# Feature-major MLP products: weights' high part against both activation parts in one 512-column pass, chunks of 256 columns

## The chip, the cores and the metric

One core of one Trainium2 chip. The metric is device time in microseconds (us), the median of several runs. PE is the matmul engine (TensorE), DVE VectorE, ACT ScalarE, POOL GpSimd, SP the engine whose queue issues the weight loads. A "pass" here is one matmul instruction: 128 x 128 weights held in the array, and so many columns streamed through them.

## The reference

A sequence of 256 tokens of width 1024 goes through a first block (mixers, then an MLP with a squared ReLU) and a second block (FFN, a hybrid mixer, FFN). The change touches the three MLP layers. Of the reference they are these lines; the rest (mixers, norms) stays as it is.

```python
x = x + jnp.square(jax.nn.relu(h @ w_mlp_in[l])) @ w_mlp_out[l]     # 1024 -> 4096 -> 1024
...
def swiglu(x, w_gate, w_up, w_down):                                 # 1024 -> 2816 -> 1024, twice
    return (jax.nn.silu(x @ w_gate) * (x @ w_up)) @ w_down
...
x = x + 0.5 * rmsnorm_2(swiglu(rmsnorm_2(x, g), w_gate, w_up, w_down), post_g)
```

All arithmetic is float32. The kernel gets that precision from fp32r matmuls by splitting each operand in a high and a low part: w·x is taken as hi·xh + hi·xl + lo·xh, three products added up in PSUM.

## The kernel before

Stages in program order: block 1's mixers, its MLP (`mlp`: W_MI, then W_MO), the first FFN (gate W_G1 and up W_U1 side by side, then down W_D1), the second mixer (`mixer2`), the second FFN (`ffn2`, the same code on W_G2, W_U2, W_D2).

**Weights.** `Wt` cuts a weight into chunks of columns (512 wide, L36) and each chunk into units of KT = 2 k-tiles, so a unit is 128 partitions x 1024 floats, 512 KB. `stream_dma` (L225) loads units in the fixed order of `plan` on SP's queue, `stream_split` (L237) makes of each raw unit a high part on ACT (L249) and a low part on DVE (L250: raw minus hi). hi and lo have 4 buffers each; a split can be issued when the last pass that reads its buffer's old content has run. `load_unit` asks for the split two units ahead and the load five ahead.

**Feature-major products** (`gemm_feat`, L320): W_MI, gate and up give their output with features on partitions and the 256 tokens as columns. For each k-tile and each 128 features f there are three passes of 256 columns: L332 (hi with xh), L334 (hi with xl), L335 (lo with xh). Two f share one PSUM bank (`acc`, [128, 2, 256]); a 512-column chunk holds two banks. As the last pass of a bank is issued, `done` takes it out: in the MLP ACT's ReLU (L990) and DVE's product with PSUM (L992), in an FFN DVE's product with the row scale rsB (L1142), ACT's SiLU (L1143) for gate, DVE's product of PSUM with it (L1147) for up; then `split_sb` makes hT's high part on ACT (L1033) and low part on DVE (L1034).

**Token-major products** (`gemm_tok`, L274): W_MO and the down products put the two token halves t = 0 and t = 1 in two banks of their own, 512 columns each: L288 (hi with h's high part), L289 (lo), L290 (hi with h's low part). For down's second chunk the last two units are run for t = 0 first and then for t = 1 (`tail=2`), so that t = 0's exit (ACT's squares L397, DVE's L1087) runs beside t = 1's passes.

**PSUM.** In these stages `banks(acc=6, tr=2)` gives six one-bank tiles for accumulators and two for transposes. A tile is taken again when all readers of its old content are through.

**Order.** SP's and POOL's orders are as written. PE, DVE and ACT are ordered by the scheduler, which interleaves neighbouring chunks where the code allows it. Each engine executes its instructions in order and stops at the first one whose wait is not met. The FFN's gate needs rsB, which at the first FFN comes out of a chain behind W_MO (x2 L1003, its squares L397, xf L1021, a Newton square root, two transposes); until rsB is there gate's results stay in PSUM.

Of the kernel before, what the change touches and what calls it, by code (L numbers as in the profile page):

```python
# [22 lines left out]
KT = 2  # L23
# [12 lines left out]
def widths_of(n):  # L36
    return [512] * (n // 512) + ([n % 512] if n % 512 else [])


class Wt:  # L40


    def __init__(self, name, k, widths):
        self.name, self.k, self.widths = name, k, widths
        self.kt = k // 128
        self.off, o = [], 0
        for w in widths:
            row = []
            for u in range(0, self.kt, KT):
                n = min(KT, self.kt - u)  # L50
# [51 lines left out]
W_MI = Wt("w_mlp_in", D, [512] * 8)  # L102
W_MO = Wt("w_mlp_out", 4096, [512] * 2)
FFW = widths_of(FF2)
W_G1 = Wt("ffn1_w_gate_2", D, FFW)
W_U1 = Wt("ffn1_w_up_2", D, FFW)
# [5 lines left out]
W_G2 = Wt("ffn2_w_gate_2", D, FFW)  # L112
W_U2 = Wt("ffn2_w_up_2", D, FFW)
# [81 lines left out]


class Prog:
# [8 lines left out]
    def plan(self):  # L206

        o = [(W_IN1, c) for c in (4, 0, 1, 3, 2, 5, 6, 7, 8)]
        for c in range(2):
            o += [(W_BRB, c), (W_BRA, c)]  # L210
        o += [(W_OUT1, 0), (W_OUT1, 1)]
        o += [(W_MI, c) for c in range(8)] + [(W_MO, 0), (W_MO, 1)]
# [24 lines left out]
    def stream_split(self, upto):  # L237

        nc = self.nc
        while self.n_split <= min(upto, len(self.units) - 1):  # L240
# [5 lines left out]
            hi = self.wh.tile([128, KT * 512], F32R, tag="hi", name="hi")  # L246
            lo = self.wl.tile([128, KT * 512], F32R, tag="lo", name="lo")
# [26 lines left out]
    def gemm_tok(self, W, c, xh, xl, done, head=0, tail=0, mid=None, late=None, rate=1, delay=0, acc=None):  # L274
# [5 lines left out]
        acc = acc or (lambda: self.pacc.tile([128, 512], F32, tag="acc", name="acc"))  # L280
        ps = [acc() for _ in range(2)]
# [152 lines left out]
    def run(self):  # L434
# [9 lines left out]
        with ExitStack() as es:  # L444
# [43 lines left out]
            with self.banks(acc=6, tr=2):  # L488
                self.ffn2(x)
# [482 lines left out]
    def mlp(self, x1):  # L972
# [11 lines left out]
        with tc.tile_pool(name="mlph", bufs=1) as hp, tc.tile_pool(name="mlpt", bufs=2) as tp:  # L984
            hT = [hp.tile([128, 32, 256], F32R, name="hT%d" % i) for i in range(2)]

            def hdone(c):
# [7 lines left out]
            for c in range(8):  # L995
                self.gemm_feat(W_MI, c, *self.x1T, hdone(c), delay=1, rate=2)
# [132 lines left out]
    def ffn(self, x, xT, rs, WG, WU, WD, gi, name, final=False):  # L1129
# [3 lines left out]
        with tc.tile_pool(name=name + "h", bufs=1) as hp, tc.tile_pool(name=name + "t", bufs=2) as tp:  # L1133
# [3 lines left out]
            for c, w in enumerate(FFW):  # L1137
                sg = {}
# [10 lines left out]
                self.gemm_feat(WG, c, *xT, gdone, delay=1, rate=2)  # L1149
                self.gemm_feat(WU, c, *xT, udone)  # L1150
# [389 lines left out]
```

## Time and profile before

| | us |
|---|---|
| median of 3 runs (least, most) | 1147.55 (1147.12, 1147.79) |
| the profiled execution | 1146.21 |
| its span in the trace | 1144.4 |
| PE busy in the span | 1117.1 |
| DVE busy | 733.1 |
| ACT busy | 553.6 |

The profile's page gives busy times and the chain of work that ended last; the trace gives groups of instructions by line (mean duration of one), a timeline (start, duration, and in brackets how long the engine had been idle and who released it), and busy time by stretches with the granted clock of PE (PEclk: 1.00 is 2.4 GHz, 0.50 is 1.2 GHz). In the trace's time the stages lie so: W_MI from 235 to 328, W_MO to 416, gate and up of the first FFN to 544, its down to 604, the second mixer to 945, gate and up of the second FFN from 948.5 to 1078, its down to 1138, the end at 1144.4. PE's matmuls are pipelined: the duration of one (0.28 us for 256 columns) is longer than the spacing of two, and the spacing is what a stream of them costs.

### The profile page before, as it was taken

What the parts mean: (1) busy time and instruction counts of PE and PEld (TensorE: products, weight loads), DVE (VectorE), ACT (ScalarE), POOL (GpSimd) and SP (SyncE); (2) the same over time, 40 slices, a digit from 0 to 9 for tenths busy, and PEclk for the clock granted to TensorE, in tenths of its full rate; (3) what the DMA queues carried; (4) which work ended last, traced back from release to release, by engine and by line L of the source; (5) the groups of instructions that cost most, each with busy time, mean ns of one, the idle gap of its engine ahead of it and who ended that gap; (6) DMA issues with size and microseconds to landing.
All of it is one profiled execution on the core that took longest, in us unless ns stands there. A gap on an engine that the chain in (4) does not pass through costs nothing.

```text
span 1144.4 us, 19495 instructions
## 1 busy us (share of the span) xinstructions
PE 1117.1 (98%) x7808; PEld 1042.9 (91%) x7808; DVE 733.1 (64%) x1155; ACT 553.6 (48%) x818; POOL 137.0 (12%) x141
## 2 busy tenths in 40 slices
PE   8987999999999999999999999999999999999997
PEld 8886899899998899999888999889999988999986
DVE  5855676766664567565557776556779777656553
ACT  6323444465553455444446335545555456444452
POOL 0411130000000000000000775000323000000000
PEclk9998999999999999999999999999999999999999
DMA  8794213655555556564754655434545565655662
GB/s 288 258 169 104 74 57 129 202 170 185 185 189 192 186 189 196 185 185 149 222 182 157 215 170 177 163 130 147 181 146 161 162 193 172 186 184 156 211 188 89
DMA packets 57035, 197.03 MB, mean 172 GB/s; under 512 B 6828, under 2 KB 7100, under 8 KB 56688
## 3 DMA queue, kind: packets, MB, share of 16 engines
q1 hardware_dynamic: 53856, 186.44, 51.1%
q0 software_dynamic: 2800, 9.21, 3.5%
q8 instruction: 61, 1.00, 0.4%
q14 instruction: 30, 0.25, 0.1%
q10 hardware_dynamic: 288, 0.14, 0.1%
HBM read 192.84 MB, written 1.44 MB: 170 GB/s over the span
## 4 chain that ended last, share of the span: by engine, by line
PE 84%; POOL 5%; DMA 5%; DVE 4%; ACT 1%; issue 1%; DVEq 0%; POOLq 0%; ACTq 0%
PE acc L332 16%; PE acc L334 16%; PE acc L335 16%; PE acc L288 9%; PE acc L290 9%; PE acc L289 9%; DMA BT<-tvd 2%; PE sm L799 2%; POOL sw L1219 2%; POOL qkT L1220 2%; DMA sw<-qkT 2%; PE o L832 1%; POOL qkT L1218 1%; DVE lo L250 1%; PE o L1341 1%
## 5 line engine op out<-in xcount | busy, mean ns | idle before, releaser
L250 DVE TENSOR_TENSOR lo<-raw,hi 128x1024 fp32r<-128x1024 f32 (+3 forms) x364 | 451.3, 1243 | 296.2 <-ACT hi L249 293.6
L249 ACT ACTIVATE hi<-raw 128x1024 fp32r<-128x1024 f32 (+3 forms) x364 | 373.0, 1026 | 446.7 <-PE acc L334 244.3
L332 PE MATMUL acc<-xh,hi 128*128 128x256 f32 x1656 | 470.9, 286 | 0.6 <-ACT hi L249 0.6
L334 PE MATMUL acc<-xl,hi 128*128 128x256 f32 x1656 | 471.0, 285 | 0.0
L335 PE MATMUL acc<-xh,lo 128*128 128x256 f32 x1656 | 469.4, 285 | 0.1
L332 PEld LDWEIGHTS acc<-xh,hi 128*128 128x128 f32 x1656 | 317.5, 192 | 4.4 <-issue 2.5
L334 PEld LDWEIGHTS acc<-xl,hi 128*128 128x128 f32 x1656 | 318.4, 192 | 2.4 <-issue 2.0
L335 PEld LDWEIGHTS acc<-xh,lo 128*128 128x128 f32 x1656 | 317.4, 192 | 1.6 <-issue 1.0
L290 PE MATMUL acc<-hi,hT 128*128 128x512 f32 x304 | 118.5, 390 | 0.0
L289 PE MATMUL acc<-lo,hT 128*128 128x512 f32 x304 | 118.3, 389 | 0.0
L288 PE MATMUL acc<-hi,hT 128*128 128x512 f32 x304 | 117.7, 389 | 0.0
L289 PEld LDWEIGHTS acc<-lo,hT 128*128 128x128 f32 x304 | 57.1, 188 | 11.9
L290 PEld LDWEIGHTS acc<-hi,hT 128*128 128x128 f32 x304 | 57.1, 188 | 11.9
L288 PEld LDWEIGHTS acc<-hi,hT 128*128 128x128 f32 x304 | 57.0, 188 | 11.4
L288 PE MATMUL acc<-hi,xh 128*128 128x386 f32 (+1 forms) x128 | 48.2, 378 | 0.9 <-ACT xh L366 0.9
L289 PE MATMUL acc<-lo,xh 128*128 128x386 f32 (+1 forms) x128 | 47.6, 372 | 0.0
L290 PE MATMUL acc<-hi,xl 128*128 128x386 f32 (+1 forms) x128 | 47.0, 373 | 0.2 <-DVE xl L367 0.2
L1038 POOL DMA_DIRECT2D row<-in_rows x4 | 2.3, 576 | 293.2 <-DVE xf L1021 214.0
L810 ACT ACTIVATE L<-L,nn 128x256 f32<-128x256 f32 (+1 forms) x48 | 21.3, 444 | 25.8 <-DVE nn L808 22.4
L288 PEld LDWEIGHTS acc<-hi,xh 128*128 128x128 f32 x128 | 24.0, 188 | 4.4 <-ACT xh L366 1.2
L290 PEld LDWEIGHTS acc<-hi,xl 128*128 128x128 f32 x128 | 24.0, 188 | 3.7 <-DVE xl L367 0.8
L289 PEld LDWEIGHTS acc<-lo,xh 128*128 128x128 f32 x128 | 24.1, 188 | 2.4
(414 smaller groups left out, 1260.1 us busy)
## 6 DMA issues: line engine op xcount, KB each, us to landing
raw<-in_w_in SPq DMA_DIRECT2D x100, 512.0 KB, 3.6
raw<-in_ffn_w_down SPq DMA_DIRECT2D x44, 512.0 KB, 4.1
raw<-in_ffn_w_gate SPq DMA_DIRECT2D x40, 512.0 KB, 3.5
raw<-in_ffn_w_up SPq DMA_DIRECT2D x40, 512.0 KB, 3.5
raw<-in_w_mlp_in SPq DMA_DIRECT2D x32, 512.0 KB, 4.2
raw<-in_w_mlp_out SPq DMA_DIRECT2D x32, 512.0 KB, 3.5
raw<-in_w_out SPq DMA_DIRECT2D x16, 512.0 KB, 3.5
raw<-in_w_in SPq DMA_DIRECT2D x16, 386.0 KB, 3.3
```

The lines of the kernel that those rows point to most:

```text
L249: nc.scalar.activation(hi[:, :n * w], raw[:, :n * w], AF.Copy)
L250: nc.vector.tensor_tensor(lo[:, :n * w], raw[:, :n * w], hi[:, :n * w], op=ALU.subtract)
L288: nc.tensor.matmul(ps[t][:, :w], xh[:, k, sl], hi, start=(k == 0), stop=False)
L289: nc.tensor.matmul(ps[t][:, :w], xh[:, k, sl], lo, start=False, stop=False)
L290: nc.tensor.matmul(ps[t][:, :w], xl[:, k, sl], hi, start=False, stop=last)
L332: nc.tensor.matmul(o, hi[:, fs], xh[:, k, :], start=(k == 0 and f % 2 == 0), stop=False, skip_group_check=True)
L334: nc.tensor.matmul(o, hi[:, fs], xl[:, k, :], start=False, stop=False, skip_group_check=True)
L335: nc.tensor.matmul(o, lo[:, fs], xh[:, k, :], start=False, stop=last, skip_group_check=True)
L799: nc.tensor.matmul(ps[:, i, :], q[pr:pr + 64, U["fts"][i], t * 128:t * 128 + 128], kk, start=True, stop=True)
L810: nc.scalar.activation(L[:, i, :], L[:, i, :], AF.Exp, bias=nn[:, i:i + 1], scale=1.0, accum_out=lsum[:, t, br, h:h + 1])
L1219: nc.gpsimd.tensor_tensor(sw, sw, bc4(1), op=ALU.mult)
L1220: nc.gpsimd.tensor_tensor(q[0:32], q[0:32], sw, op=ALU.add)
```

## The change

W_MI, gate and up use a new function, `gemm_pair`, in the place of `gemm_feat` (which stays for the mixers). The two parts of the activations now lie side by side in one tile `xs` [128, 8, 2, 256] (`Parts`), so hi can meet both in one pass of 512 columns (L368); lo with xh stays a pass of 256 columns (L369). The accumulator is a tile of two banks, one for each f; within a bank the first 256 columns collect hi·xh + lo·xh and the others hi·xl. At the exit ACT copies the second halves to an SBUF tile `sum` (L373), DVE adds the first halves (L374), and the old steps work on `sum`. Chunks are 256 columns wide and units four k-tiles of 256 columns, so the bytes of a unit and the number of units stay. In these stages all accumulators are two-bank tiles, three of them; `gemm_tok` takes t = 0 and t = 1 as the two banks of one tile. `sum` and `sg` have two buffers each.

```diff
-W_MI = Wt("w_mlp_in", D, [512] * 8)
+W_MI = Wt("w_mlp_in", D, [256] * 16, 4)
-FFW = widths_of(FF2)
+FFW = [256] * (FF2 // 256)
...
+class Parts:
+    def __init__(self, both):
+        self.both = both
+        self.hi, self.lo = both[:, :, 0, :], both[:, :, 1, :]
...
     def gemm_tok(...)
-        acc = acc or (lambda: self.pacc.tile([128, 512], F32, tag="acc", name="acc"))
-        ps = [acc() for _ in range(2)]
+        if self.pair:
+            ps = self.pacc.tile([128, 2, 512], F32, tag="acc", name="acc")
+            ps = [ps[:, 0, :], ps[:, 1, :]]
+        else:
+            acc = acc or (lambda: self.pacc.tile([128, 512], F32, tag="acc", name="acc"))
+            ps = [acc() for _ in range(2)]
...
+    def gemm_pair(self, W, c, x, done, rate=1, delay=0):
+        nc = self.nc
+        ps = self.pacc.tile([128, 2, 512], F32, tag="acc", name="acc").rearrange("p f (a t) -> p f a t", a=2)
+        for u in range(len(W.off[c])):
+            for k, hi, lo in self.load_unit(W, c, u):
+                last = k == W.kt - 1
+                for f in range(2):
+                    fs = slice(f * 128, f * 128 + 128)
+                    nc.tensor.matmul(ps[:, f, :, :], hi[:, fs], x.both[:, k, :, :], start=(k == 0), stop=False)
+                    nc.tensor.matmul(ps[:, f, 0, :], lo[:, fs], x.hi[:, k, :], start=False, stop=last)
+                if delay <= k < W.kt - 1:
+                    self.flush(rate)
+        s = self.sump.tile([128, 2, 256], F32, tag="sum", name="sum")
+        nc.scalar.activation(s, ps[:, :, 1, :], AF.Copy)
+        nc.vector.tensor_tensor(s, ps[:, :, 0, :], s, op=ALU.add)
+        done(s)
...
-            with self.banks(acc=6, tr=2):
+            with self.banks(acc=3, tr=2, pair=True):
...
-                def f(i, ps):
-                    r = tp.tile([128, 2, 256], F32, tag="r", name="r")
-                    nc.scalar.activation(r, ps, AF.Relu)
+                def f(p):
                     h = tp.tile([128, 2, 256], F32, tag="h", name="h")
-                    nc.vector.tensor_tensor(h, ps, r, op=ALU.mult)
-                    self.split_sb(h, hT, 4 * c + 2 * i)
+                    nc.vector.scalar_tensor_tensor(h, p, 0.0, p, op0=ALU.max, op1=ALU.mult)
+                    self.split_sb(h, hT, 2 * c)
...
-                def gdone(i, ps):
-                    s = sg[i] = tp.tile([128, 2, 256], F32, tag="s%d" % i, name="s")
-                    nc.vector.tensor_tensor(s, ps, bc2, op=ALU.mult)
-                    nc.scalar.activation(s, s, AF.Silu)
+                def gdone(p):
+                    nc.vector.tensor_tensor(p, p, bc2, op=ALU.mult)
+                    nc.scalar.activation(sg, p, AF.Silu)
-                def udone(i, ps):
+                def udone(p):
                     h = tp.tile([128, 2, 256], F32, tag="h", name="h")
-                    nc.vector.tensor_tensor(h, ps, sg[i], op=ALU.mult)
-                    self.split_sb(h, hT, 4 * c + 2 * i)
+                    nc.vector.tensor_tensor(h, p, sg, op=ALU.mult)
+                    self.split_sb(h, hT, 2 * c)
```

How the change moves instructions is seen at three places. The first is PE's order in the first FFN's gate and up, at the join of two chunks. In the rows of before acc_4560 is the second bank of the first up chunk (u0) and acc_4689 the first bank of the second gate chunk.

```order
L332 MATMUL acc_4560<-xh_3731,hi_4591 128x256
L334 MATMUL acc_4560<-xl_3732,hi_4591 128x256
L335 MATMUL acc_4560<-xh_3731,lo_4592 128x256
L332 MATMUL acc_4689<-xh_3731,hi_4621 128x256 [waits Activation_49]
L334 MATMUL acc_4689<-xl_3732,hi_4621 128x256
L335 MATMUL acc_4689<-xh_3731,lo_4622 128x256
```

After, two such joins in PE's order. acc_4290 is the second gate chunk (g1), acc_4340 the second up chunk (u1, in the tile that held g0), acc_4393 the third gate chunk (g2), acc_4443 the third up chunk (u2, in the tile that held g1).

```order
L368 MATMUL acc_4290<-xs_3489,hi_4260 128x512
L369 MATMUL acc_4290<-xs_3489,lo_4261 128x256
L368 MATMUL acc_4340<-xs_3489,hi_4291 128x512 [waits DVE_49]
L369 MATMUL acc_4340<-xs_3489,lo_4292 128x256
...
L368 MATMUL acc_4393<-xs_3489,hi_4363 128x512
L369 MATMUL acc_4393<-xs_3489,lo_4364 128x256
L368 MATMUL acc_4443<-xs_3489,hi_4394 128x512 [waits DVE_49,PE_49]
L369 MATMUL acc_4443<-xs_3489,lo_4395 128x256
```

Three passes for a weight tile became two, and the first pass of u1 and of u2 now waits for DVE, where before it waited for ACT's split alone. The second place is DVE's order at the same point of the program, from the split before rsB on. Before (acc_4403 and acc_4404 are the first gate chunk's two banks, s its scaled copies):

```order
L250 TENSOR_TENSOR lo_4692<-raw_4595,hi_4691 128x1024 [waits DMAHW6_49,PE_49,Activation_49]
L513 COPY rsB_4394<-tr_4485 128x256 [waits PE_49]
L1142 TENSOR_TENSOR s_4547<-acc_4403,rsB_4394 128x512 [waits DVE_49]
L1142 TENSOR_TENSOR s_4556<-acc_4404,rsB_4394 128x512
L250 TENSOR_TENSOR lo_4722<-raw_4625,hi_4721 128x1024 [waits DMAHW7_49,PE_49,Activation_49]
L1147 TENSOR_TENSOR h_4675<-acc_4559,s_4547 128x512 [waits Activation_49]
L1147 TENSOR_TENSOR h_4685<-acc_4560,s_4556 128x512 [waits Activation_49]
```

After (sum_4232 is g0's sum, sum_4282 u0's, sum_4335 g1's; lo_4467 goes into the buffer that g2's last pass reads):

```order
L263 TENSOR_TENSOR lo_4445<-raw_4367,hi_4444 128x1024 [waits DMAHW0_49,Activation_49]
L1178 TENSOR_TENSOR sum_4232<-sum_4232,rsB_4149 128x512 [waits DVE_49]
L263 TENSOR_TENSOR lo_4467<-raw_4398,hi_4466 128x1024 [waits DMAHW1_49,PE_49,Activation_49]
L1183 TENSOR_TENSOR h_4285<-sum_4282,sg_4158 128x512 [waits Activation_49]
L374 TENSOR_TENSOR sum_4335<-acc_4290,sum_4335 128x512 [waits DVE_49,Activation_49]
L1178 TENSOR_TENSOR sum_4335<-sum_4335,rsB_4149 128x512 [waits DVE_49]
```

The read that frees g1's accumulator (L374) stands behind the split lo_4467 and behind h; before, the reads that free the gate's banks stood right behind rsB. The third place is PE's order at the end of the first FFN's down product, where the passes for t = 0 end and those for t = 1 begin. Before:

```order
L288 MATMUL acc_6093<-hi_6239,hT0_4401 128x512
L289 MATMUL acc_6093<-lo_6240,hT0_4401 128x512
L290 MATMUL acc_6093<-hi_6239,hT1_4402 128x512
L288 MATMUL acc_6094<-hi_6221,hT0_4401 128x512
L289 MATMUL acc_6094<-lo_6222,hT0_4401 128x512
```

After:

```order
L305 MATMUL acc_5536<-hi_5681,hT0_4156 128x512
L306 MATMUL acc_5536<-lo_5682,hT0_4156 128x512
L307 MATMUL acc_5536<-hi_5681,hT1_4157 128x512
L305 MATMUL acc_5536<-hi_5663,hT0_4156 128x512 [waits DVE_49]
L306 MATMUL acc_5536<-lo_5664,hT0_4156 128x512
```

The order of the passes is the same, but both halves are one tile now, and the first pass for t = 1 waits for a read of t = 0's half by DVE. The same wait stands in the second FFN's down product. At W_MO's end the scheduler put the last three t = 1 passes, which have this wait too, behind 26 passes of the first FFN.

## Rows read from the trace of the kernel before

**Rows 1.** The page, part 1: engine, busy us, share of the span, instructions.

```profile
PE 1117.1 (98%) x7808; PEld 1042.9 (91%) x7808; DVE 733.1 (64%) x1155; ACT 553.6 (48%) x818; POOL 137.0 (12%) x141
```

**Rows 2.** Windows by stage: us, busy by engine, PEclk, DMA share, GB/s.

```profile
235.00:328.00 93.00, 93.00 (x776) 92.96 (x777) 58.42 (x67) 51.85 (x69) 0.00 (x0) 1.00 0.57 183
416.00:544.00 128.00, 128.00 (x1069) 128.00 (x1069) 82.11 (x117) 64.26 (x82) 0.65 (x2) 1.00 0.56 178
544.00:604.00 60.00, 60.00 (x267) 49.62 (x266) 31.11 (x33) 27.01 (x34) 0.00 (x0) 1.00 0.64 200
948.50:1078.20 129.70, 129.70 (x1069) 129.70 (x1070) 79.72 (x105) 64.80 (x82) 0.00 (x0) 0.99 0.56 173
```

**Rows 3.** Timeline of PE in gate and up: start us, duration us, engine, line.

```profile
460.78 0.28 PE L334 MATMUL acc<-xl,hi 128*128 128x256 f32 x1
...
461.74 0.28 PE L332 MATMUL acc<-xh,hi 128*128 128x256 f32 x1
```

**Rows 4.** Timeline of PE in the first down product, 512 columns.

```profile
579.66 0.39 PE L290 MATMUL acc<-hi,hT 128*128 128x512 f32 x1
...
581.02 0.39 PE L290 MATMUL acc<-hi,hT 128*128 128x512 f32 x1
```

**Rows 5.** Groups by line and shape: busy us, mean ns of one, idle before.

```profile
L250 DVE TENSOR_TENSOR lo<-raw,hi 128x1024 fp32r<-128x1024 f32 x324 | 411.4, 1272 | 270.0 <-ACT hi L249 267.6 <-PE acc L335 0.6 <-PE sm L363 0.6
L249 ACT ACTIVATE hi<-raw 128x1024 fp32r<-128x1024 f32 x324 | 343.2, 1060 | 407.0 <-PE acc L334 220.6 <-PE acc L290 113.2 <-issue 47.9
L1147 DVE TENSOR_TENSOR h<-acc,s 128x512 f32<-128x512 f32 x22 | 15.1, 689 | 2.7 <-PE acc L335 1.7 <-ACT s L1143 0.7
L990 ACT ACTIVATE r<-acc 128x512 f32<-128x512 f32 x16 | 9.4, 589 | 10.3 <-PE acc L335 10.3
```

**Rows 6.** Timeline of ACT and DVE as the first FFN's first SiLU comes.

```profile
440.22 1.06 ACT L249 ACTIVATE hi<-raw 128x1024 fp32r<-128x1024 f32 x1 [2.26 <-PE acc L334]
441.30 1.28 ACT L1143 ACT_TABLE_LOAD   x1
442.60 1.15 ACT L1143 ACTIVATE s<-s 128x512 f32<-128x512 f32 x2
...
441.32 1.23 DVE L250 TENSOR_TENSOR lo<-raw,hi 128x1024 fp32r<-128x1024 f32 x1 [0.44 <-ACT hi L249]
```

**Rows 7.** Timeline at the first FFN's start, DVE's chain towards rsB.

```profile
415.54 1.40 DVE L1003 SCALAR_TENSOR_TENSOR x<-acc,r,x 128x512 f32<-128x512 f32 x2
...
424.50 2.48 DVE L1021 SCALAR_TENSOR_TENSOR xf<-x,rf,row 128x1024 f32<-128x1024 f32 x2
```

**Rows 8.** Timeline at the end of the first down product.

```profile
600.97 0.39 PE L288 MATMUL acc<-hi,hT 128*128 128x512 f32 x1
...
601.17 0.69 ACT L397 ACTIVATE junk<-acc,rsf 128x512 bf16<-128x512 f32 x1 [1.87 <-PE acc L290]
...
602.06 0.74 DVE L1087 SCALAR_TENSOR_TENSOR f<-acc,rsf,row 128x512 f32<-128x512 f32 x1
```

**Rows 9.** Timeline at the end of the second down product.

```profile
1135.35 0.39 PE L288 MATMUL acc<-hi,hT 128*128 128x512 f32 x1
...
1136.44 0.74 DVE L1087 SCALAR_TENSOR_TENSOR f<-acc,n_r,row 128x512 f32<-128x512 f32 x1
```

**Rows 10.** Timeline at the start of the second mixer.

```profile
605.04 0.44 PE L288 MATMUL acc<-hi,xh 128*128 128x386 f32 x1 [0.86 <-ACT xh L366]
...
605.76 0.34 DVE L367 SCALAR_TENSOR_TENSOR xl<-acc,cols,xh 128x128 fp32r<-128x128 f32 x1
...
607.89 0.33 PE L363 MATMUL tr<-ident,xn 128*128 128x128 f32 x1 [0.39 <-DVE xn L1104]
```

**Rows 11.** Windows around pauses of PE: us, PE busy, then the clock as PEclk.

```profile
945.00:948.50 3.50, 1.39 (x7) 0.62 (x6) 3.46 (x10) 2.24 (x9) 0.64 (x2) 1.00 0.58 206
949.40:952.70 3.30, 3.30 (x18) 3.30 (x17) 2.70 (x6) 2.00 (x4) 0.00 (x0) 0.50 0.06 22
...
603.90:607.90 4.00, 2.51 (x14) 1.71 (x12) 3.66 (x10) 2.84 (x8) 0.00 (x0) 1.00 0.01 2
607.90:611.00 3.10, 3.10 (x19) 2.60 (x20) 2.67 (x8) 2.01 (x6) 1.51 (x3) 1.00 0.56 191
```

More of the change, by code (lines that the diff above doesn't have):

```diff
@@ L48, in __init__ @@
             row = []
-            for u in range(0, self.kt, KT):
-                n = min(KT, self.kt - u)
+            for u in range(0, self.kt, kts):
+                n = min(kts, self.kt - u)
                 row.append((o, u, n))
@@ L211, in plan @@
         o += [(W_OUT1, 0), (W_OUT1, 1)]
-        o += [(W_MI, c) for c in range(8)] + [(W_MO, 0), (W_MO, 1)]
+        o += [(W_MI, c) for c in range(len(W_MI.widths))] + [(W_MO, 0), (W_MO, 1)]
         def ffn(g, u, d):
@@ L231, in stream_dma @@
             w = W.widths[c]
-            raw = self.wr.tile([128, KT * 512], F32, tag="raw", name="raw")
+            raw = self.wr.tile([128, UNIT], F32, tag="raw", name="raw")
             nc.sync.dma_start(raw[:, :n * w], self.ap[W.name][o:o + 128 * n * w].rearrange("(p f) -> p f", p=128))
@@ L380, in new_xT @@
     def new_xT(self):
-        return (self.xtp.tile([128, 8, 256], F32R, tag="xh", name="xh"),
-                self.xtp.tile([128, 8, 256], F32R, tag="xl", name="xl"))
+        return Parts(self.xtp.tile([128, 8, 2, 256], F32R, tag="xs", name="xs"))
     def held(self, on):
@@ L416, in banks @@
     @contextmanager
-    def banks(self, acc, tr, sm=0, o=0):
+    def banks(self, acc, tr, sm=0, o=0, pair=False):
+        self.pair = pair
         with ExitStack() as es:
@@ L487, in run @@
             self.dump("x4", x)
-            with self.banks(acc=6, tr=2):
+            with self.banks(acc=3, tr=2, pair=True):
                 self.ffn2(x)
@@ L985, in mlp @@
             hT = [hp.tile([128, 32, 256], F32R, name="hT%d" % i) for i in range(2)]
+            self.sump = tp
             def hdone(c):
-                def f(i, ps):
-                    r = tp.tile([128, 2, 256], F32, tag="r", name="r")
-                    nc.scalar.activation(r, ps, AF.Relu)
+                def f(p):
                     h = tp.tile([128, 2, 256], F32, tag="h", name="h")
-                    nc.vector.tensor_tensor(h, ps, r, op=ALU.mult)
-                    self.split_sb(h, hT, 4 * c + 2 * i)
-                return f
-            for c in range(8):
-                self.gemm_feat(W_MI, c, *self.x1T, hdone(c), delay=1, rate=2)
+                    nc.vector.scalar_tensor_tensor(h, p, 0.0, p, op0=ALU.max, op1=ALU.mult)
+                    self.split_sb(h, hT, 2 * c)
+                return f
+            for c in range(len(W_MI.widths)):
+                self.gemm_pair(W_MI, c, self.x1T, hdone(c), delay=1, rate=2)
             xT = self.new_xT()
@@ L1136, in ffn @@
             bc2 = rsB.unsqueeze(1).to_broadcast([128, 2, 256])
-            for c, w in enumerate(FFW):
-                sg = {}
-                def gdone(i, ps):
-                    s = sg[i] = tp.tile([128, 2, 256], F32, tag="s%d" % i, name="s")
-                    nc.vector.tensor_tensor(s, ps, bc2, op=ALU.mult)
-                    nc.scalar.activation(s, s, AF.Silu)
-                def udone(i, ps):
+            self.sump = tp
+            for c in range(len(FFW)):
+                sg = tp.tile([128, 2, 256], F32, tag="sg", name="sg")
+                def gdone(p):
+                    nc.vector.tensor_tensor(p, p, bc2, op=ALU.mult)
+                    nc.scalar.activation(sg, p, AF.Silu)
+                def udone(p):
                     h = tp.tile([128, 2, 256], F32, tag="h", name="h")
-                    nc.vector.tensor_tensor(h, ps, sg[i], op=ALU.mult)
-                    self.split_sb(h, hT, 4 * c + 2 * i)
-                self.gemm_feat(WG, c, *xT, gdone, delay=1, rate=2)
-                self.gemm_feat(WU, c, *xT, udone)
+                    nc.vector.tensor_tensor(h, p, sg, op=ALU.mult)
+                    self.split_sb(h, hT, 2 * c)
+                self.gemm_pair(WG, c, xT, gdone, delay=1, rate=2)
+                self.gemm_pair(WU, c, xT, udone)
             return self.down_post(WD, hT, gi, x, 0.5, name, rs, None if final else self.g["mix_pre_g_2"])
```

25 lines of the change are left out of this document (14 added, 11 removed).

## The prediction, made before the changed kernel ran

> **What bounds the kernel now.** I read the page's busy times first: PE is busy 98% of the span, DVE and ACT about two thirds and half of it [rows 1]. Shares over the span hide stages, so the windows by stage come next: in W_MI, in gate and up of both FFNs and in the first down product PE is busy in every microsecond, at full clock, while DVE has a third of its time free and ACT nearly half, at 173 to 200 GB/s of weights [rows 2]. So there the price is PE's spacing of passes, not a split or a load, and only two things can move the end: fewer PE nanoseconds, or a new wait of PE that no other passes cover.
>
> **What it removes.** Nine passes in PE's timeline of gate and up show 8 spacings in 461.74 - 460.78 = 0.96 us: 0.120 us for 256 columns [rows 3]. Seven 512-column passes show 6 spacings in 581.02 - 579.66 = 1.36: 0.227 us [rows 4]. Two 256-column passes cost 0.240, one of 512 costs 0.227: each pass has about 13.3 ns that don't grow with its columns (256 columns at 2.4 GHz are 106.7 ns). A weight tile cost 3 x 0.120 = 0.360 us and will cost 0.227 + 0.120 = 0.347. W_MI has 8 k-tiles x 32 groups of 128 features = 256 of them, each FFN 8 x 44 = 352, in all 960: **-12.8 us**. That is all there is to gain, since the columns streamed stay the same.
>
> The Trainium skill ("TensorE: Matmul & The Clock Gate", section Back-to-back issue gap) speaks against this: it gives an isolated pass N/2.4 + 2.5 ns, so a fixed part of 2.5 ns instead of 13.3. By that the merged pass would save about 2.4 us, an estimate from the Trainium skill's figure, and the sum below would be 10.4 us worse. Its other figure, 131 ns for 512 columns in a stream, is contradicted here by 227 ns [rows 4]. The rival on the saving below takes it up from rows.
>
> **What it adds on ACT and DVE.** Per chunk of 256 columns one ACT copy out of PSUM (nearest row: ReLU from PSUM, 0.59 us) and one DVE add of the same shape as h (0.69) [rows 5]. A gate chunk with its up chunk takes PE 32 x 0.347 = 11.1 us; in it DVE has 4 splits at 1.27 and five 512-wide operations at 0.69, 8.5 us, and ACT 4 splits at 1.06 and four operations of about 0.6, 6.6 us [rows 5]. Both fit, with a quarter of DVE's time free. Units stay 512 KB and come every 2.78 us, as slow as in the down products, so loads cost nothing. With three two-bank tiles a chunk's exit has the next two chunks' passes, 11.1 us, before its tile is wanted; it takes 0.59 + 0.69 plus one split (1.27) that may stand ahead. In the steady stream I charge nothing; if that cover were gone, each of 60 chunks could pay up to 1.3 us.
>
> **Where it adds waits that nothing covers.** By the order, at three kinds of places.
>
> (a) First FFN's start, first passes of g1. The scheduler runs g0, u0 and g1 interleaved, and puts W_MO's last three t = 1 passes among them. g1's first low part goes into the buffer that W_MO's last pass frees; from then on hi 1.06, lo 1.27 and handoffs of 0.15 are needed [rows 5], 2.5 us, while about 10 passes (1.7 us) stand between. Stall 0.8 us; ends 0 and 2.5.
>
> (b) u1's first pass wants g0's tile. DVE's read of it (L374) stands behind a split whose buffer is freed by g0's last pass: hi 1.06, lo 1.27, sum 0.69 and 0.28 of handoffs, 3.3 us [rows 5], against 8 passes or 1.4 us. At least 1.9 us. DVE also has the chain towards rsB here, x2 and xf of 1.40 and 2.48 us [rows 7], which comes later than before because W_MO's end is late; I take 2.5, ends 1.9 and 5.
>
> (c) u2's first pass wants g1's tile, and there is no pass between g2's last one and it. DVE's read of g1 stands behind the split lo_4467 (freed by that last pass) and behind h, which needs SiLU. On ACT follow one another: hi 1.06, the table load 1.28, SiLU 0.58 [rows 6], the copy of g1 0.59; then DVE's sum 0.69 [rows 5]; with five handoffs of 0.06, 4.5 us, all of it stall. Ends: 3 (if the copy or the load comes earlier in time) and 6.
>
> In the trace the SiLU starts 20 ns after the table load ends, and the load has 1.28 us [rows 6]. The Trainium skill ("ScalarE: Activation LUTs", section What ACT_TABLE_LOAD costs) has the load at 1283 ns, which the row confirms, and a drain of about 1380 ns besides, which the row doesn't show ahead of SiLU; by the Trainium skill (c) would be 1.4 us longer and the whole about 1150.0.
>
> (d) The ends of the two down products. t = 0 and t = 1 are one tile now, and t = 1's first pass waits for DVE's read of t = 0. In the trace it starts at 600.97, ACT's squares at 601.17 and DVE's read L1087 from 602.06 to 602.80 [rows 8]: with 0.05 for the handoff 602.85 - 600.97 = 1.88 us. The second FFN's has the same shape, 1135.35 to 1136.44 + 0.74 + 0.05 [rows 9]: 1.88. The exit behind it follows PE in both, so nothing takes it back: **3.8 us**. (A wait for ACT's squares alone would give 0.9 each.)
>
> (e) Starts of the second mixer and the second FFN. The first passes there wait for DVE's low part, not ACT's high part. In the mixer the first pass starts at 605.04 and the low part that it would wait for ends at 606.10, 1.1 us later; but PE waits at 607.89 for xn all the same [rows 10], which swallows most of it. I take 0.2 and for the FFN 0.3, ends 0 and 1.7 together.
>
> (f) The clock. After the 3.5 us around 945 in which PE was busy for 1.39, the granted clock went to 0.50 for 3.3 us; after 4 us with 2.51 busy it stayed at 1.00 [rows 11]. The stall of 4.5 us in (c) is more like the first: 3.3 us at half rate lose 1.65. I charge one, **1.7 us**; ends 0 and 5.
>
> **Sum.** -12.8 + 0.8 + 2.5 + 4.5 + 3.8 + 0.5 + 1.7 = +1.0 us. The profiled execution took 1146.2 and its span 1144.4, the median is 1147.55, 1.3 above the former; a difference carries over, so 1147.3 for an execution like it and **1148.6 us** for the median. All low ends at once (0, 1.9, 3.0, 1.8, 0, 0) give 1141.4, all high ones (2.5, 5, 6, 3.8, 1.7, 5) 1158.7. One of (b), (c) and (f) at an end moves the sum by 1.5 to 3.3, so the forecast's own range is 1145.3 to 1150.5.
>
> **Rivals.**
> *Slower, the start of the first FFN decides.* One engine queue holds splits, sums and the chain to rsB. If W_MO's late end delays x2 and xf, each 2.48 us of xf stands ahead of the sum for u1, and (b) and (a) pause PE long enough for the clock too. Price: two more half-rate stretches of 1.65, 3.3 us more, about 1152. For it: PE is the only engine that has no slack and its pauses follow each other within 20 us. Against: after 1.5 us of idle within 4 us the clock held [rows 11]. It decides from about 2.3 us over the forecast's waits.
> *Faster, the waits are half.* I read the waits at the FFN's start off the order; a wait on an engine counts everything before it, and if splits get ahead in time because ACT and DVE have free time, (a) to (c) and the clock cost 4 to 5 us less: about 1144.5. For it: a quarter of DVE's time is free. Against: buffers freed by PE's own last passes fix (b) and (c).
> *All waits hidden.* Only the -12.8 and perhaps the tails: 1134.8 to 1138.5. Against: the tile shared by t = 0 and t = 1 can't be hidden by anything in the rows.
> *The saving is not there.* If the fixed 13 ns goes with the switch of weights and a 512-column pass followed by a 256-column one waits for it differently than in equal streams, the 12.8 shrinks to 2 or so: 1159. Rows 3 and 4 show only streams of equal passes. The gap rule of the Trainium skill, cited above, leads to the same time.
>
> **Chances.** Forecast 0.48 (1145.3 to 1150.5); slower start 0.25 (1150.5 to 1154); half waits 0.15; all hidden 0.05; saving not there 0.07. 0.2% is 2.3 us, about what a measurement here can tell from none: same lies between 1145.25 and 1149.85. Slower: 0.24 + 0.07 + 0.06 of the forecast's own upper end, 0.37. Faster: 0.13 + 0.05 + 0.03, 0.21. Same 0.42. The range from 1141.5 to 1154.0 leaves out the last two rivals and an edge of the others.
>
> **What would show it.** Spacing of PE in gate and up of 0.227 and 0.120 alternately, and W_MI's window shorter by 256 x 13.3 ns = 3.4 us, the second FFN's gate and up by 4.7. At the first FFN's start idle times of PE ahead of L368, released by DVE's L374, of about 2.5 and 4.5 us, and a stretch at 0.50 behind the second. In both down products an idle of 1.9 us ahead of L305, released by DVE. DVE's and ACT's own durations as before. I am wrong if the alternating spacing is above 0.36 us for a pair, if PE idles in the steady stream, or if the first FFN's start loses under 4 or over 12 us.

## The result and the profile after

The changed kernel took 1152.25 us (median of 15 runs), the kernel before 1145.47 (15 runs): ratio 1.0066, 95% interval 1.0050 to 1.0081. It is slower by two thirds of a per cent. The time lies inside the wide range of the prediction (1141.5 to 1154.0), but above the forecast's own 1145.3 to 1150.5, where the rival "slower, the start of the first FFN decides" lies. The likeliest case, no change that can be told, is not what came.

The profiled execution took 1152.25 with a span of 1150.5. Its busy times, which answer to [rows 1]:

```profile
PE 1114.8 (97%) x6848; PEld 995.0 (86%) x6848; DVE 769.6 (67%) x1207; ACT 573.0 (50%) x854; POOL 137.0 (12%) x141
```

PE has 960 instructions less and is busy 2.3 us less, but the span is 6.0 us longer. A table of the stages, each from its first pass to the next stage's first pass, shows where (us; the last column is the best version of the experiments below):

| stage | before | after | best |
|---|---|---|---|
| W_MI | 92.9 | 89.6 | 89.9 |
| W_MO | 88.1 | 87.4 | 88.1 |
| first FFN, gate and up | 128.0 | 136.3 | 125.2 |
| first down, to the mixer's first pass | 61.2 | 64.4 | 61.2 |
| second mixer | 343.4 | 345.1 | 344.5 |
| second FFN, gate and up | 129.7 | 127.0 | 126.7 |
| second down, to the start of its last pass | 59.6 | 61.7 | 59.6 |
| from there to the end of the span | 6.6 | 7.1 | 7.1 |
| sum from W_MI's start | 909.5 | 918.5 | 902.4 |

In the column "after" three passes of W_MO, 0.8 us with their pause, are counted with gate and up. From W_MI's start on the changed kernel is 9.0 us longer; block 1 ahead of it, in code that is the same, happened to be 3 us shorter in this execution (more on that at the last experiment).

Windows by stage (us, busy by engine, PEclk, DMA share, GB/s), which answer to [rows 2] and [rows 11]:

```profile
232.00:321.50 89.50, 89.50 (x518) 78.36 (x519) 68.51 (x83) 51.46 (x69) 0.00 (x0) 1.00 0.59 189
409.00:545.00 136.00, 129.32 (x719) 111.58 (x718) 96.95 (x136) 74.49 (x99) 0.65 (x2) 0.97 0.54 176
954.70:1081.60 126.90, 126.90 (x717) 110.36 (x717) 92.53 (x120) 74.02 (x97) 0.00 (x0) 0.99 0.56 183
441.90:446.30 4.40, 0.08 (x1) 0.00 (x0) 2.63 (x5) 4.21 (x6) 0.00 (x0) 0.90 0.64 189
446.40:452.20 5.80, 5.80 (x18) 4.93 (x19) 4.36 (x7) 2.75 (x5) 0.00 (x0) 0.50 0.08 33
```

W_MI and the second FFN are still full of PE. The first FFN's gate and up has 6.7 us without PE, and PE ran at 0.50 of its clock for 5.8 us behind a pause of 4.4 us. PE's waits (us in total, times, longest) name the releasers:

```profile
PE acc L368 <- DVE sum L374: 6.0, 2, 4.4
PE acc L305 <- DVE f L1123: 3.4, 2, 1.7
...
PE acc L305 <- DVE xs L403: 2.0, 1, 2.0
```

These are the predicted waits: L368 on DVE's read of an accumulator twice, the two down products' t = 1 passes on DVE's read of t = 0, and the second mixer's first pass on DVE's instruction for the low part (L403; what it waits for there is taken up below, at (e)). The longest, in the timeline of PE, DVE and ACT:

```profile
439.81 0.42 DVE L549 COPY rsB<-tr 128x256 f32<-128x256 f32 x1 [1.67 <-PE tr L548]
...
441.70 0.28 PE L369 MATMUL acc<-xs,lo 128*128 128x256 f32 x1
446.39 0.77 PE L368 MATMUL acc<-xs,hi 128*128 128x512 f32 x1 [4.42 <-DVE sum L374]
...
442.98 1.23 DVE L263 TENSOR_TENSOR lo<-raw,hi 128x1024 fp32r<-128x1024 f32 x1 [1.02 <-ACT hi L262]
444.92 0.69 DVE L1183 TENSOR_TENSOR h<-sum,sg 128x512 f32<-128x512 f32 x1 [0.72 <-ACT sg L1179]
445.55 0.69 DVE L374 TENSOR_TENSOR sum<-acc,sum 128x512 f32<-128x512 f32 x1
...
441.89 1.06 ACT L262 ACTIVATE hi<-raw 128x1024 fp32r<-128x1024 f32 x1 [2.19 <-PE acc L368]
442.97 1.28 ACT L1179 ACT_TABLE_LOAD   x1
444.26 0.63 ACT L1179 ACTIVATE sg<-sum 128x512 f32<-128x512 f32 x1
444.92 0.60 ACT L373 ACTIVATE sum<-acc 128x512 f32<-128x512 f32 x1
```

g2's last pass starts at 441.70, u2's first at 446.39: 4.69 us where a spacing is 0.12, so 4.57 lost. Between them stand, one behind the other, hi, the table load, SiLU, h beside the copy of g1, and DVE's sum, as (c) had them. The pause of the first down product, which answers to [rows 8]:

```profile
602.14 0.39 PE L307 MATMUL acc<-hi,hT 128*128 128x512 f32 x1
...
603.45 0.74 DVE L1123 SCALAR_TENSOR_TENSOR f<-acc,rsf,row 128x512 f32<-128x512 f32 x1
...
604.25 0.50 PE L305 MATMUL acc<-hi,hT 128*128 128x512 f32 x1 [1.73 <-DVE f L1123]
```

2.11 us from pass to pass instead of 0.227: 1.88 lost, the second down product's 2.11 (1138.56 to 1140.67) the same.

What the merged pass gave is read from starts of passes far apart. In W_MI, 58 pairs of a 512 and a 256 pass, and in the first FFN 57:

```profile
269.85 0.40 PE L368 MATMUL acc<-xs,hi 128*128 128x512 f32 x1
...
289.96 0.40 PE L368 MATMUL acc<-xs,hi 128*128 128x512 f32 x1
```

```profile
479.83 0.40 PE L368 MATMUL acc<-xs,hi 128*128 128x512 f32 x1
...
499.97 0.40 PE L368 MATMUL acc<-xs,hi 128*128 128x512 f32 x1
```

20.11 / 58 = 346.7 ns, as predicted, and 20.14 / 57 = 353.3 ns. Three passes of 256 cost 360 [rows 3]. So W_MI saves 13.3 ns for a weight tile, the FFNs (the second has 353 as well) only 6.7.

### The profile page after: what moved, and what is told of

It is laid out like the page before. It is cut to its first block, busy times and chain, and to the rows that moved or that the text cites. A ratio compares the mean times of both kernels' runs of the same rounds, so it can differ in the third digit from the quotient of the medians.

```text
span 1150.5 us, 17641 instructions
## 1 busy us (share of the span) xinstructions
PE 1114.8 (97%) x6848; PEld 995.0 (86%) x6848; DVE 769.6 (67%) x1207; ACT 573.0 (50%) x854; POOL 137.0 (12%) x141
## 4 chain that ended last, share of the span: by engine, by line
PE 84%; POOL 5%; DMA 4%; DVE 4%; ACT 2%; issue 1%; DVEq 0%; SPq 0%; POOLq 0%; ACTq 0%
PE acc L368 19%; PE acc L369 10%; PE acc L305 9%; PE acc L306 9%; PE acc L307 9%; PE acc L349 6%; PE acc L351 6%; PE acc L352 6%; PE sm L835 2%; POOL sw L1255 2%; DMA sw<-qkT 2%; POOL qkT L1256 2%; DMA BT<-tvd 1%; PE o L868 1%; POOL qkT L1254 1%; DVE lo L263 1%
## 5 line engine op out<-in xcount | busy, mean ns | idle before, releaser
L263 DVE TENSOR_TENSOR lo<-raw,hi 128x1024 fp32r<-128x1024 f32 (+2 forms) x356 | 450.7, 1269 | 270.9 <-ACT hi L262 268.9
L262 ACT ACTIVATE hi<-raw 128x1024 fp32r<-128x1024 f32 (+2 forms) x356 | 371.1, 1044 | 439.1 <-issue 132.7
L368 PE MATMUL acc<-xs,hi 128*128 128x512 f32 x960 | 342.6, 401 | 6.2 <-DVE sum L374 6.0
L369 PE MATMUL acc<-xs,lo 128*128 128x256 f32 x960 | 270.1, 282 | 0.7 <-DVE lo L263 0.7
L368 PEld LDWEIGHTS acc<-xs,hi 128*128 128x128 f32 x960 | 181.9, 190 | 50.5 <-issue 4.7
L349 PE MATMUL acc<-xs,hi 128*128 128x256 f32 (+1 forms) x696 | 199.7, 288 | 0.3 <-ACT hi L262 0.3
L351 PE MATMUL acc<-xs,hi 128*128 128x256 f32 (+1 forms) x696 | 198.9, 287 | 0.0
L352 PE MATMUL acc<-xs,lo 128*128 128x256 f32 (+1 forms) x696 | 198.0, 287 | 0.1
L369 PEld LDWEIGHTS acc<-xs,lo 128*128 128x128 f32 x960 | 182.9, 191 | 1.3 <-DVE lo L263 1.0
L349 PEld LDWEIGHTS acc<-xs,hi 128*128 128x128 f32 (+1 forms) x696 | 133.4, 192 | 3.7 <-issue 2.5
L351 PEld LDWEIGHTS acc<-xs,hi 128*128 128x128 f32 (+1 forms) x696 | 133.7, 192 | 2.4 <-issue 2.0
L352 PEld LDWEIGHTS acc<-xs,lo 128*128 128x128 f32 (+1 forms) x696 | 132.9, 192 | 1.6 <-issue 1.0
L305 PE MATMUL acc<-hi,hT 128*128 128x512 f32 x304 | 118.7, 391 | 3.4 <-DVE f L1123 3.4
L305 PEld LDWEIGHTS acc<-hi,hT 128*128 128x128 f32 x304 | 57.1, 188 | 16.1 <-DVE f L1123 4.3
L306 PEld LDWEIGHTS acc<-lo,hT 128*128 128x128 f32 x304 | 57.1, 188 | 11.7
L305 PE MATMUL acc<-hi,xs 128*128 128x386 f32 (+1 forms) x128 | 48.6, 381 | 2.1 <-DVE xs L403 2.0
L374 DVE TENSOR_TENSOR sum<-acc,sum 128x512 f32<-128x512 f32 x60 | 41.1, 684 | 0.0
```

What stands on the lines that cost most here:

```text
L262: nc.scalar.activation(hi[:, :n * w], raw[:, :n * w], AF.Copy)
L263: nc.vector.tensor_tensor(lo[:, :n * w], raw[:, :n * w], hi[:, :n * w], op=ALU.subtract)
L305: nc.tensor.matmul(ps[t][:, :w], xh[:, k, sl], hi, start=(k == 0), stop=False)
L306: nc.tensor.matmul(ps[t][:, :w], xh[:, k, sl], lo, start=False, stop=False)
L349: nc.tensor.matmul(o, hi[:, fs], xh[:, k, :], start=(k == 0 and f % 2 == 0), stop=False, skip_group_check=True)
L351: nc.tensor.matmul(o, hi[:, fs], xl[:, k, :], start=False, stop=False, skip_group_check=True)
```

## The experiments

Four edits of the changed kernel alone, run side by side; then two combinations, one narrower edit, and the kernel before once more. Medians are of 6 to 15 runs. The versions did not all run on the same chip, so each ratio is against the kernel before on its own chip.

| version | median us | ratio, 95% interval |
|---|---|---|
| changed kernel | 1152.25 | 1.0066, 1.0050 to 1.0081 |
| two tiles in three places | 1139.96 | 0.9951, 0.9933 to 0.9968 |
| four buffers for sum | 1146.22 | 1.0003, 0.9986 to 1.0020 |
| order 512, 512, 256, 256 | 1149.72 | 1.0031, 1.0017 to 1.0044 |
| merged pass undone | 1156.26 | 1.0090, 1.0066 to 1.0114 |
| two tiles for W_MO alone | 1144.09 | 0.9992, 0.9974 to 1.0009 |
| two tiles, order 512, 512, 256, 256 | 1136.32 | 0.9918, 0.9898 to 0.9938 |
| all three edits | 1137.58 | 0.9925, 0.9896 to 0.9953 |

**Two tiles for the two token halves.** In the second chunk of W_MO and of both down products:

```diff
-            ps = self.pacc.tile([128, 2, 512], F32, tag="acc", name="acc")
-            ps = [ps[:, 0, :], ps[:, 1, :]]
+            ps = [self.pacc.tile([128, 2, 512], F32, tag="acc", name="acc") for _ in range(1 + c)]
+            ps = [ps[0][:, 0, :], ps[c][:, 1 - c, :]]
```

> The changed kernel with one edit: in the second chunk of W_MO and of the down products, the token halves t = 0 and t = 1 lie in two accumulator tiles instead of in the two banks of one. Theory (a tile is one unit for waits): the idle of 1.88 us ahead of the first t = 1 pass goes in both down products, 3.8 us of the span, and at W_MO's end the last three t = 1 passes stand where they stood before, with no pause among the first FFN's first passes (0.95 us today). Total 3 to 5 us shorter than the changed kernel, about 1148. Rival (the exit behind the last pass, not the wait, sets the end; or two tiles more in use delay the next chunk): the idle moves to the first passes of the next chunk or to the exit, and the total stays within 1 us of 1152.

It took 12.3 us off, not 3 to 5. The waits of L305 on DVE's f are gone, as expected (2.0 us each with the passes' slow start), and the mixer's first pass waits for ACT's high part again:

```profile
PE acc L368 <- DVE sum L374: 1.0, 1, 1.0
PE acc L305 <- ACT xs L402: 0.9, 1, 0.9
```

But the first row shows more: of the 6.0 us of PE's waits for DVE's reads at the first FFN's start 1.0 is left. Gate and up took 127.0 us (417.57 to 544.52) where the changed kernel had 136.3, and no stretch is at 0.50. So 8.5 us of the first FFN's loss (136.3 less W_MO's 0.8, less 127.0) hung on the shared tile as well. The expectation had missed that; which of the three places does it is the question of the fifth experiment.

**Four buffers for sum** in the FFNs:

```diff
-        with ... as hp, tc.tile_pool(name=name + "t", bufs=2) as tp:
+        with ... as hp, tc.tile_pool(name=name + "t", bufs=2) as tp, \
+                tc.tile_pool(name=name + "s", bufs=4) as sp:
...
-            self.sump = tp
+            self.sump = sp
```

> The changed kernel with one edit: the tile sum has four buffers in the FFNs instead of two. In the changed kernel PE waits 4.58 us at 441.7 for DVE's read of the second gate chunk's accumulator. Theory A (the buffers): that read can't be issued because the sum's two buffers are held by the first gate and up chunks until rsB has come; with four buffers it is done long before, the idle of 4.6 us goes, and with it the 5.7 us at half clock behind it (2.6 to 3 us lost); total about 7.5 us shorter, near 1144.7. Theory B (the prediction's: the splits in front of it in DVE's queue and ACT's table load): the splits and the load stay, so at least 2 us of the idle stays and the half clock may too; total 0 to 3 us shorter.

6.0 us off by the medians; gate and up took 129.0 us instead of 136.3, and the pause of 4.6 us and the half clock are gone: theory A. DVE's reads of g0, u0 and g1 (L374) now stand ahead of rsB in time, where the changed kernel had g1's at 445.55, 5.7 us behind rsB:

```profile
426.91 0.68 DVE L374 TENSOR_TENSOR sum<-acc,sum 128x512 f32<-128x512 f32 x1
428.71 0.69 DVE L374 TENSOR_TENSOR sum<-acc,sum 128x512 f32<-128x512 f32 x1
430.51 0.69 DVE L374 TENSOR_TENSOR sum<-acc,sum 128x512 f32<-128x512 f32 x1
...
438.54 0.42 DVE L549 COPY rsB<-tr 128x256 f32<-128x256 f32 x1
```

The splits, the table load and SiLU are still there; PE just doesn't wait for them. So what the prediction called the cause of (c), a split and the table load in front of the read, only set how long after rsB the read came. That it had to come after rsB is due to two buffers, both held by sums that wait for rsB.

**Another order of the passes:** both of 512 columns of a k-tile, then both of 256.

```diff
                     nc.tensor.matmul(ps[:, f, :, :], hi[:, fs], x.both[:, k, :, :], start=(k == 0), stop=False)
+                for f in range(2):
+                    fs = slice(f * 128, f * 128 + 128)
                     nc.tensor.matmul(ps[:, f, 0, :], lo[:, fs], x.hi[:, k, :], start=False, stop=last)
```

> The changed kernel with the four passes of a k-tile in another order: both 512-column passes first, then both of 256 columns. In the changed kernel a 512 and a 256 pass together take 346.7 ns in W_MI, as predicted, but 353.3 in both FFNs. Theory A (the extra 6.6 ns come from alternating the two lengths): in this order the pair costs 227 + 120 = 347 ns everywhere, the FFNs give 704 x 6.6 = 4.7 us. Theory B (they come from the stage, by what it reads, or by the state in which the stream was left by a stall): 353 ns stay in the FFNs and 347 in W_MI, total unchanged within 1.5 us.

2.5 us off by the medians, 4.0 by the ratios. A pair costs 348.3 to 348.6 ns in all three stages in this order, so neither theory holds whole: the FFNs gain 5 ns for a pair (704 x 5 = 3.5 us), W_MI loses 1.6 (0.4 us). The other half of theory B, the state in which the stream was left by a pause, gets its evidence from the two-tile version, where the alternating order stayed. There W_MI's 57 pairs, the same instructions in the same order as in the changed kernel, took this:

```profile
269.78 0.40 PE L368 MATMUL acc<-xs,hi 128*128 128x512 f32 x1
...
289.92 0.40 PE L368 MATMUL acc<-xs,hi 128*128 128x512 f32 x1
```

20.14 / 57 = 353.3 ns. So it is not the stage: the alternating stream has two rhythms, 346.7 and 353.3. In each of the four profiles with that order the rhythm changed only where something broke the alternation, and then held, for up to 100 us. That can be a pause or a few transposes, but also two passes of one length in a row, with PE never idle. In the two-tile version's second FFN six pairs from 955.85 to 957.97 took 353.3 ns each; then the scheduler put passes of one length side by side at several places, with no idle time of PE, and the 18 pairs behind them took 6.24 us, 346.7 ns each:

```profile
958.32 0.64 PE L368 MATMUL acc<-xs,hi 128*128 128x512 f32 x2
...
965.33 0.39 PE L368 MATMUL acc<-xs,hi 128*128 128x512 f32 x1
...
971.57 0.39 PE L368 MATMUL acc<-xs,hi 128*128 128x512 f32 x1
```

What picks a rhythm at such a place is not settled.

**The merged pass undone alone**, all else as changed:

```diff
-                    nc.tensor.matmul(ps[:, f, :, :], hi[:, fs], x.both[:, k, :, :], start=(k == 0), stop=False)
+                    nc.tensor.matmul(ps[:, f, 0, :], hi[:, fs], x.hi[:, k, :], start=(k == 0), stop=False, ...)
+                    nc.tensor.matmul(ps[:, f, 1, :], hi[:, fs], x.lo[:, k, :], start=False, stop=last, ...)
```

> The changed kernel with the merged pass undone alone: hi meets the activations' high and low part in two passes of 256 columns again, into the same two halves of the same banks; chunks, tiles, exits and waits stay as in the changed kernel. It isolates what the merged pass is worth. Theory (13.3 ns of each pass don't grow with its columns): three passes take 360 ns, 13.3 more than in W_MI and 6.7 more than in the FFNs, 3.4 + 4.7 = 8.1 us, total about 1160. Rival (the merge gains nothing on the whole, because the stream's end is set by waits): total within 2 us of 1152.

4.0 us more by the medians, half of the 8.1. The intervals of the two ratios overlap, so the totals alone don't prove the gain; the stages do. The passes are spaced by 0.120 again, W_MI takes 92.9 and the second FFN's gate and up 130.0, 3.3 and 3.0 us more than in the changed kernel. The rest went the other way in the first FFN's gate and up, 132.1 us against 136.3:

```profile
PE acc L368 <- DVE sum L377: 2.8, 2, 1.5
...
440.94 1.06 ACT L262 ACTIVATE hi<-raw 128x1024 fp32r<-128x1024 f32 x1 [2.27 <-PE acc L370]
442.01 1.28 ACT L1182 ACT_TABLE_LOAD   x1
...
443.61 0.28 PE L372 MATMUL acc<-xs,lo 128*128 128x256 f32 x1
445.44 0.36 PE L368 MATMUL acc<-xs,hi 128*128 128x256 f32 x1 [1.55 <-DVE sum L377]
```

The longest pause is 1.5 us instead of 4.4 and no half clock follows it. This isn't a slower stream that meets the same waits later: g2's last pass starts 32.3 us into the stage, in the changed kernel 32.8. The table load came earlier, 30.7 us into the stage instead of 34.1, with four of ACT's splits between the copy of u0 and it where the changed kernel has five. So the engines' order is another in this version, and in this stage the edit doesn't isolate the merge.

Read the other way: from W_MI's start to the end this version takes 921.2 us against 909.5 before, so the chunks, two-bank tiles and exits without the merge cost 11.7 us. The merge gives 2.7 of that back in these profiles.

**Two tiles for W_MO alone**, the down products as changed:

```diff
+            two = int(c == 1 and W is W_MO)
+            ps = [self.pacc.tile([128, 2, 512], F32, tag="acc", name="acc") for _ in range(1 + two)]
+            ps = [ps[0][:, 0, :], ps[two][:, 1 - two, :]]
```

> The changed kernel with two accumulator tiles for the second chunk of W_MO alone; both down products keep t = 0 and t = 1 in one tile. With two tiles in all three places the total fell by 12.3 us, of which the two down products' waits explain 3.8 and the first mixer pass 1.1. Theory (W_MO's shared tile is the root of the first FFN's loss: it moves the last three t = 1 passes, and so x2 and the chain to rsB, 5 us back, and rsB late holds sum's buffers and with them the second gate chunk's accumulator): this edit alone takes 7 to 9 us off the first FFN's gate and up, its idle of 4.6 us and the half clock behind it go, total about 1144.5. Rival (the scheduler's other order in the three-place version did it, by something in the down products): the idle of 4.6 us ahead of L368 stays, total near 1152.

8.2 us off, with the down products' waits still there. Gate and up took 127.0 us at full clock, and the chain to rsB begins and ends earlier:

```profile
408.20:535.20 127.00, 125.96 (x718) 109.30 (x717) 96.06 (x135) 73.98 (x99) 0.65 (x2) 1.00 0.54 187
```

```profile
407.93 1.40 DVE L1040 SCALAR_TENSOR_TENSOR x<-acc,r,x 128x512 f32<-128x512 f32 x2
...
427.50 0.41 DVE L550 COPY rsB<-tr 128x256 f32<-128x256 f32 x1
```

Both x2 steps run back to back here, and rsB's copy comes 19.6 us later; in the changed kernel the last x2 came at 414.40, 5.1 us behind the first, and rsB 25.4 us after that. So the theory holds: the loss of 8 us in the first FFN starts at W_MO's shared tile, which the scheduler answered by moving three passes behind 26 others.

**Two tiles and the other order; and all three edits.**

> Two accumulator tiles in all three second chunks, and the passes of a k-tile in the order 512, 512, 256, 256. In the alternating order the pair of a 512 and a 256 pass took 346.7 ns or 353.3 ns, each held from one pause of PE to the next; in this order it took 348.3 in all three stages. Theory (two patterns of the alternating stream, chosen at a pause): here 348.3 ns everywhere, so against the two-tile version with 353.3 in all three stages 960 x 5 = 4.8 us less, about 1135 to 1136. Rival (what a pass saves is taken back by a wait elsewhere): total within 1.5 us of 1140.

> The three edits together: two tiles in the second chunks, four buffers for sum in the FFNs, passes in the order 512, 512, 256, 256. With two tiles PE still waits 1.25 us for DVE's read of an accumulator at the first FFN's start. Theory (that wait is for sum's buffers too): it goes, total 1 to 1.3 us under the version without the four buffers, about 1134.5. Rival (it is the split in front of the read): the wait stays, no difference.

The first gave 1136.32, 3.6 us under two tiles alone (3.8 by the ratios), with the same cost of a pair in W_MI and in the FFN (56 pairs each; x2 marks two passes in one row):

```profile
270.20 0.62 PE L368 MATMUL acc<-xs,hi 128*128 128x512 f32 x2
...
289.71 0.62 PE L368 MATMUL acc<-xs,hi 128*128 128x512 f32 x2
```

```profile
479.99 0.63 PE L368 MATMUL acc<-xs,hi 128*128 128x512 f32 x2
...
499.49 0.62 PE L368 MATMUL acc<-xs,hi 128*128 128x512 f32 x2
```

348.4 and 348.2 ns. The theory asked for 4.8 us; the stages show 1.2, 1.8 and 1.0, together 4.0. It is faster than both kernels, by 0.8% than the one before. Adding the four buffers gave nothing more (1137.58, intervals overlapping); PE's wait for DVE's read of an accumulator is 0.9 us in both:

```profile
PE acc L368 <- DVE sum L376: 0.9, 1, 0.9
```

So that last wait is not for sum's buffers. That it is the split in front of the read was argued from the order, not tried.

**The kernel before again.**

> The kernel before, profiled once more. The wait of PE for gek in block 1 (about 81 us into the span) took 11.3 us in its first profile and 6.4 to 9.6 in the five profiles of the changed kernel and its variants, in code that the change leaves as it was. If it varies from run to run, it is another value here, and the span differs from the first by as much; if the change shortens it, it is above 10 again.

Its wait for gek in block 1 is the shortest of all, so it varies from run to run; these are the rows of its first profile and of the second:

```profile
PE sm L730 <- DVE gek L721: 11.1, 1, 11.1
```

```profile
PE sm L730 <- DVE gek L721: 5.9, 1, 5.9
```

The span did not follow it: 1145.2 against 1144.4, W_MI's start at 235.4 against 234.9, since other times in block 1 moved too. From W_MI's start on the two profiles of before agree, 909.8 and 909.5 us. Over the eight profiles with the change W_MI's start lies between 229.6 and 238.3. This is why the stages were compared from W_MI on.

## Why the prediction was right where it was, and wrong where it was

| term | forecast us | measured us |
|---|---|---|
| saving in W_MI, 256 weight tiles | -3.4 | -3.3 |
| saving in both FFNs, 704 weight tiles | -9.4 | -4.7 |
| (a) g1's first low part | 0.8 | 1.1 |
| (b) u1's first pass | 2.5 | 1.9 |
| (c) u2's first pass | 4.5 | 4.6 |
| (d) two down products, with the slow first passes behind them | 3.8 | 4.0 |
| (e) first passes of mixer and second FFN | 0.5 | 0.8 |
| (f) half clock | 1.7 | 2.6 |
| behind the last pass | 0 | 0.6 |
| sum | 1.0 | 7.6 |

The 1.4 us that remain to 9.0 were not followed up. The second mixer alone varies by as much: its length is 343.4 and 344.1 us in the two profiles of before and 343.7 to 346.4 in those with the change. The 0.6 behind the last pass stands in all versions with the change and has no explanation either.

**That the time lies in the wide range is partly luck.** The forecast was added to a median of before of 1147.55 us, from 3 runs; beside the changed kernel the median of before was 1145.47. The change is 6.8 us, where the sum said 1.0 and the range ended 6.45 us over its own base (1154.0 less 1147.55).

**The saving is the step that failed.** 13.3 ns for each pass was read from two streams of equal passes [rows 3, 4] and carried to a stream that alternates. In W_MI it held; in the FFNs the alternating stream ran in its slower rhythm, and half of 9.4 us was not there. The prediction had named this ("rows 3 and 4 show only streams of equal passes") as a rival of 0.07 that takes nearly all the saving; 4.8 of the 12.8 us went. The Trainium skill ("TensorE: Matmul & The Clock Gate", section Back-to-back issue gap) has a fixed part of 2.5 ns for an isolated pass, which makes 5 ns for a pair, an estimate. Neither rhythm agrees with it: over 320 ns for 768 columns at 2.4 GHz a pair costs 26.7 or 33.3 ns more here.

**The waits (a) to (d) were right in place and nearly in size**: all lie between the instructions named. That both sums are 11.6 is luck, since (b) came 0.6 shorter and (a), (c) and (d) 0.1 to 0.3 longer. For (c) the working was right in time and incomplete in cause. That the read stood behind a split and a table load was true of the order, but the order was a consequence: sum's two buffers were held until rsB, and rsB was late because W_MO's shared tile delayed x2. The rival "slower, the start of the first FFN decides" said that the late end of W_MO delays x2; it looked for the price in longer (a) and (b), and it was in (c). In SiLU's start the trace agrees with [rows 6] again: 444.26, where the table load ends at 444.25. The drain that the Trainium skill adds ("ScalarE: Activation LUTs", section What ACT_TABLE_LOAD costs) is again not seen.

**The clock** was charged too little. The pause of 4.4 us did bring 0.50, but for 5.8 us, where the row it was taken from had 3.3 [rows 11]: the 18 passes in that stretch take 3.2 us at full rate, so 2.6 were lost.

**(e) was 0.3 too low, and its reason fails in the mixer.** The second FFN's first pass came 0.8 us later (the stretch from the mixer's W_OUT2 to it is 26.5 us against 25.7). Ahead of it PE waits 0.6 us at a transpose for the instruction that writes the low part; undoing the merge, which lets that first pass take the high part alone, gave 25.7 again. In the mixer the first pass came 1.1 us later, and shorter pauses behind it gave that back, as forecast: its first 256-column pass starts 12.1 us behind the last down pass in both kernels. But it doesn't need the low part. With two tiles in all three places it started before any low part was written, with two tiles for W_MO alone while the first was being written; these are the rows of the two versions, in this order:

```profile
605.73 0.44 PE L305 MATMUL acc<-hi,xs 128*128 128x386 f32 x1 [0.86 <-ACT xs L402]
606.19 0.34 DVE L403 SCALAR_TENSOR_TENSOR xs<-tr,cols,xs 128x128 fp32r<-128x128 f32 x1
```

```profile
598.85 0.34 DVE L404 SCALAR_TENSOR_TENSOR xs<-tr,cols,xs 128x128 fp32r<-128x128 f32 x1
599.07 0.41 PE L306 MATMUL acc<-hi,xs 128*128 128x386 f32 x1 [1.54 <-DVE f L1124]
```

In the changed kernel it started right behind the L403 that reads a transpose out of an accumulator tile:

```profile
609.21 0.34 DVE L403 SCALAR_TENSOR_TENSOR xs<-acc,cols,xs 128x128 fp32r<-128x128 f32 x1
609.61 0.45 PE L305 MATMUL acc<-hi,xs 128*128 128x386 f32 x1 [1.96 <-DVE xs L403]
```

So it probably waits there for the last reader of the accumulator that it takes over, another one in each version; that was not tried by itself.

**The steady stream** held: no idle of PE in gate and up of the second FFN nor in W_MI, with DVE's busy time up from 58 to 69 us in W_MI and 80 to 93 in the second FFN [rows 2]. The copies and adds at the exit cost nothing there.

So the direction was missed by the saving's size first (4.8 of the 6.6 us between the sums), then by the clock (0.9), the end (0.6) and (e) (0.3). None of the prediction's signs of being wrong appeared (0.353 us for a pair, no idle in the steady stream, 10.2 us lost at the first FFN's start by (a), (b), (c) and (f)): they were too wide to catch half the saving.

## What to carry to other kernels

A fixed cost per pass that is read from a stream of equal passes is an estimate for a stream of mixed ones; keep its half as a case, and try an order that puts equal passes side by side. A tile of two banks is one thing to wait for: halves that are read and written at different times belong in tiles of their own, above all where the read starts a chain (here x2 to rsB) that later frees other buffers. An edit of a few passes can move the order on every engine (here three passes of W_MO, a split of ACT), so compare stage by stage before a difference in time is put down to the edit.

## What the runs showed of the hardware

Alternating passes of 512 and 256 columns ran in one of two rhythms, 346.7 or 353.3 ns for the pair, in the same instructions of the same stage in different versions; the rhythm changed only where a pause, a few transposes or two passes of one length in a row broke the alternation. Within the faster one the spacings were 230 to 233 and 112 to 118 ns by turns, in the slower 232 to 241 and 113 to 120, repeating every three pairs. In the order 512, 512, 256, 256 a pair cost 348.2 to 348.6 ns in every stage looked at. After a pause of 4.4 us the granted clock was 0.50 for 5.8 us; after three pauses of 1.9 us and less (ahead of 429.99, 604.25 and 1140.67 in the changed kernel) it stayed at 1.00.
